# Branch and output projections of a hybrid layer as three float32r passes, with their splits between the merges

## The chip, the cores and the metric

The kernel runs on one core of a Trainium2 chip. The metric is the device time of one execution in microseconds; before the change the median of three runs is 1143.91 us (1143.75 to 1143.92).

## The reference

One layer over 256 tokens of width 1024, all in float32. One input projection gives queries, keys, values and a forget gate for an attention of eight heads, the channels of a pooling branch and of a state-space branch, and three gates per channel. The part that is changed joins the branches:

```
gates  = sigmoid(g)                                   # (256, 3, 1024)
merged = (gates[0] * (y_a @ w_branch_a)               # 512 -> 1024
        + gates[1] * (y_b @ w_branch_b)               # 256 -> 1024
        + gates[2] * (y_c @ w_branch_c))              # 256 -> 1024
mix = merged @ w_out                                  # 1024 -> 1024
x = layer_norm(alpha * x + mix)
x = layer_norm(alpha * x + moe(x))                    # top 4 of 32 experts
```

The mixture of experts reads all weights of all 32 experts, 384 chunks of 1 MiB. They are nearly all of the 438 MB that the kernel loads.

## The kernel before

**The ring.** SBUF holds 24 slots of 128x2048 float32, 1 MiB each. Weights come as chunks, one to a slot, in the order in which they are used: the input projection, then the eight chunks of the branch weights (`CH_BR`) and the output weights (`CH_WO`) in turn, then the experts. A slot that is released (`release`, `done`, `drop`) is at once given to the next chunk by `load_more` (L109), which puts one load into the queue of SyncE. That queue works in order, so a load waits for those ahead of it, and for the last reader of its slot. A buffer that isn't a chunk (the branch inputs, three tiles of gates, x itself) takes a slot with `keep` and gives it back with `drop`. Twelve slots are working space of the trunk at first; three of them (`f_spl`) hold the parts of split weights.

**Splits.** For the value, pooling and gate projections (the list `SPLIT`) a weight half of 128x1024 is split in two: ScalarE copies it as float32r (L235), VectorE subtracts that from the original (L236), and `mm3` (L250 to L252) multiplies in three float32r matmuls: high by high, high by low, low by high. Every projection of a half calls `split_next` behind its matmuls, which writes the parts three halves ahead, into the buffer that was just read.

**Stages.** Up to 156 us the trunk projects; attention, pooling and the state-space scan run on the other engines between. Then comes the part around the change. `branch(d)`, for d from 0 to 7, makes 128 of the 1024 merged channels: eight float32 products with the branch inputs `yv(k)` (L770) in PSUM tiles `pab` and `pcc`, and on VectorE the merge with the gates (L779, L780, L784, L785) into a tile `m`. `mixk` multiplies one `m` with its rows of the output weights, in four float32 products of 512 columns (L791) that add up in four PSUM tiles `mix` over d. The order in the code is branch 0, branch 1, mix 0, branch 2, mix 1, and so on, with the last two mixes at the end. In between stand the router's weights (GpSimd, L799), their sum over the rows (VectorE, L802), and the load of an activation table for Sqrt (ScalarE, L823). The layer norm and the routing follow, and from 224 us on the experts, two at a time, in 16 rounds of 24 chunks.

Of the kernel before, what the change touches and what calls it, by code (L numbers as in the profile page):

```python
# [17 lines left out]
S = 256  # L18
# [36 lines left out]
CH_V = [6, 7]  # L55
CH_UP = 8
CH_G = list(range(9, 21))
CH_BR = [21, 23, 25, 27]
CH_WO = [22, 24, 26, 28]
N_TRUNK = 29  # L60


@with_exitstack
def hybrid_layer(ctx: ExitStack, tc: tile.TileContext, wt, wm, pa, pb, pc, xin, bu, lnp, b_down, out):
    nc = tc.nc
    pe, act, dve, pool, sp = nc.tensor, nc.scalar, nc.vector, nc.gpsimd, nc.sync
    TT, TS, STT = dve.tensor_tensor, dve.tensor_scalar, dve.scalar_tensor_tensor
# [51 lines left out]
    def chunk(i):  # L119
        return chunks[i][0]  # L120

    def done(i):
        f = chunks.pop(i)[1]
        release(f)
# [4 lines left out]
    def a_(n):  # L129
        return pa_sb[:, PA[n][0]:PA[n][1]]  # L130
# [12 lines left out]
    epst = con.tile([128, 2], F32)  # L143
# [3 lines left out]
    junk = scr[:, 0:1]  # L147
# [47 lines left out]
    big = {}  # L195
# [10 lines left out]
    def drop(name):  # L206
        release(big.pop(name)[1])
# [2 lines left out]
    def gate_tile(i, n=1):  # L210
        return big[f"gates{i // 8}"][0].rearrange("p (u t) -> p u t", u=8)[:, i % 8:i % 8 + n]

    def yv(k, n=1):
        return big["y"][0].rearrange("p (k t) -> p k t", k=8)[:, k:k + n]

    def work(f):
        return place(f).rearrange("p (i q t) -> p i q t", i=4, q=2)

    SPLIT = CH_V + [CH_UP] + CH_G
    jobs = [(c, h) for c in SPLIT for h in range(2)]
    js = {"emitted": 0, "used": 0}
    parts = {}

    def split_next():
        j = js["emitted"]
        if j >= len(jobs):
            return
        js["emitted"] += 1  # L230
        ci, h = jobs[j]
        src = chunk(ci)[:, h * 1024:(h + 1) * 1024]
        t = place(f_spl[j % 3], F32R)
        hi, lo = t[:, 0:1024], t[:, 1024:2048]
        act.activation(out=hi, in_=src, func=ACTF.Copy)  # L235
        TT(lo, src, hi.bitcast(F32), op=ALU.subtract)  # L236
        parts[j] = (hi, lo)
        if h:
            done(ci)

    def split(ci, h):
        j = js["used"]
        js["used"] += 1
        assert jobs[j] == (ci, h)
        while js["emitted"] <= j:
            split_next()
        return parts.pop(j)

    def mm3(out, whi, wlo, ahi, alo, first, last):
        pe.matmul(out, whi, ahi, start=first, stop=False)  # L250
        pe.matmul(out, whi, alo, start=False, stop=False)  # L251
        pe.matmul(out, wlo, ahi, start=False, stop=last)  # L252
# [146 lines left out]


    def proj(ci, half, dst):
        if ci in SPLIT:
            hi, lo = split(ci, half)
            for k in range(8):
                mm3(dst, hi[:, k * 128:(k + 1) * 128], lo[:, k * 128:(k + 1) * 128], xhi[:, k], xlo[:, k], k == 0, k == 7)
            split_next()
        else:
            w = chunk(ci)[:, half * 1024:half * 1024 + 1024]
            for k in range(8):
                pe.matmul(dst, w[:, k * 128:(k + 1) * 128], xt3[:, k], start=(k == 0), stop=(k == 7))  # L410
            if half:
                done(ci)

    def pair_tile():
        return pm.tile([128, 2, S], F32, tag="m", name="pm")
# [90 lines left out]
    def s5_sigmoid():  # L506
        y, t, g, sg = s5st["post"]
        hb = sm("hb", 2)
        TS(hb, a_("b_glu"), 0.5, None, op0=ALU.mult)
        for m in range(2):  # L510
            act.activation(out=sg[:, m], in_=s5st["glu"][:, m], func=ACTF.Tanh, scale=0.25, bias=hb[:, m:m + 1])
        STT(t, sg, 1.0, g, op0=ALU.add, op1=ALU.mult)
        TS(yv(6, 2), t, 0.25, None, op0=ALU.mult)
        release(f_s0)


# [21 lines left out]
    def pool_out():  # L538
        mx = s5st["mx"]
        pp = pst.tile([128, 2, S], F32, tag="t", name="pp")  # L540
        wp = b_("w_pool").rearrange("p (j d) -> p j d", j=2)
        for j in range(2):
            pe.matmul(pp[:, j, :], wp[:, j, :], mx[:, j, :], start=True, stop=True)
        for j in range(2):
            TS(yv(4 + j)[:, 0], pp[:, j], a_("p_scale")[:, j:j + 1], None, op0=ALU.mult)
        release(f_s1)


# [43 lines left out]
    def att_pv(i):  # L592
        po = pst.tile([128, S], F32, tag="t", name="po")
        for part in range(2):
            for q in range(2):
                h = 2 * i + q
                PT = ast["T", h]
                o = po[64 * q:64 * q + 64]
                v = vsb[:, part, h * 64:(h + 1) * 64]
                if part == 0:  # L600
                    pe.matmul(o, v, PT[:, 0:256], start=True, stop=False)
                else:
                    pe.matmul(o[:, 128:256], v, PT[:, 256:384], start=False, stop=True)
        act.activation(out=yv(i)[:, 0], in_=po, func=ACTF.Copy)


    pus = pair_tile()
# [40 lines left out]
    def at(n, f, *a):  # L648
        side.setdefault(n, []).append((f, a))
# [46 lines left out]
    at(21, s5_out, 2)  # L696
    at(25, s5_out, 3)
    steps(s5_fwd, 0, 7, 7, 8, 8, 9, 9, 10, 10)
    at(6, keep, "y")
    at(9, keep, "gates0")  # L700
    steps(s5_fwd, 1, 11, 11, 12, 12, 13, 13, 14, 14)
    steps(s5_fwd, 2, 15, 15, 16, 16, 17, 17, 18, 18)
# [16 lines left out]
    for i in range(4):  # L719
        p = pair_tile()  # L720
# [14 lines left out]
    for g in range(12):  # L735
        if g in (3, 7):
            keep(f"gates{g // 4 + 1}")
        p = pair_tile()
# [4 lines left out]
    ph1.close()  # L743
    release(f_xhi)
    release(f_xlo)
    for f in f_spl:
        release(f)


    late = ctx.enter_context(tc.tile_pool(name="late", bufs=1, reuse_waits="tile"))  # L750
# [1 line left out]
    rbias = late.tile([128, 2, NE], F32)  # L752
    wrp = ExitStack()
    wr2 = wrp.enter_context(tc.tile_pool(name="wrp", bufs=1, side="right", reuse_waits="tile")).tile([128, 2, 8, NE], F32, name="wr2")
# [3 lines left out]
    pbr = ps2.enter_context(tc.tile_pool(name="pbr", bufs=2, space=PSUM, reuse_waits="tile"))  # L758
    pmx = ps2.enter_context(tc.tile_pool(name="pmx", bufs=1, space=PSUM, reuse_waits="tile"))
    wk2 = ps2.enter_context(tc.tile_pool(name="wk2", bufs=2, reuse_waits="tile"))  # L760
    mix = [[pmx.tile([128, 512], F32, name=f"mix{t}{n}") for n in range(2)] for t in range(2)]
    mst = {}

    def branch(d):
        w = chunk(CH_BR[d // 2])[:, d % 2 * 1024:d % 2 * 1024 + 1024]
        pab = pbr.tile([128, 2, S], F32, tag="ab", name="pab")
        pcc = pbr.tile([128, S], F32, tag="c", name="pcc")
        for dst, k0, k1 in ((pab[:, 0], 0, 4), (pab[:, 1], 4, 6), (pcc, 6, 8)):
            for k in range(k0, k1):
                pe.matmul(dst, w[:, k * 128:(k + 1) * 128], yv(k)[:, 0], start=(k == k0), stop=(k == k1 - 1))  # L770
        if d % 2:
            done(CH_BR[d // 2])

        t = wk2.tile([128, 3, S], F32, tag="mg", name="mg")
        if d == 5:
            STT(t[:, 0:1], gate_tile(15), 1.0, pab[:, 0:1], op0=ALU.add, op1=ALU.mult)
            STT(t[:, 1:2], gate_tile(16), 1.0, pab[:, 1:2], op0=ALU.add, op1=ALU.mult)
        else:
            STT(t[:, 0:2], gate_tile(3 * d, 2), 1.0, pab, op0=ALU.add, op1=ALU.mult)  # L779
        STT(t[:, 2:3], gate_tile(3 * d + 2), 1.0, pcc[:, None], op0=ALU.add, op1=ALU.mult)  # L780
        if d in (2, 5, 7):
            drop(f"gates{(d - 1) // 3 if d > 2 else 0}")
        m = wk2.tile([128, S], F32, tag="m", name="m", bufs=3)
        TT(t[:, 0], t[:, 0], t[:, 1], op=ALU.add)  # L784
        TT(m, t[:, 0], t[:, 2], op=ALU.add)  # L785
        mst[d] = m

    def mixk(*parts):
        for k, t, n in parts:
            w = chunk(CH_WO[k // 2])[:, k % 2 * 1024 + n * 512:k % 2 * 1024 + n * 512 + 512]  # L790
            pe.matmul(mix[t][n], mst[k][:, t * 128:(t + 1) * 128], w, start=(k == 0), stop=(k == 7))  # L791
            if (k % 2, t, n) == (1, 1, 1):
                done(CH_WO[k // 2])


    def router_weights():
# [2 lines left out]
            pool.tensor_tensor(wr2[:, i], wr2[:, 1], l1[:, 8 * i:8 * i + 8, None].to_broadcast([128, 8, NE]), op=ALU.mult)  # L799

    def router_reduce():
        dve.tensor_reduce(rbias, wr2.rearrange("p a k e -> p a e k"), axis=AX.X, op=ALU.add)  # L802

    def router_sums():
        pr = pbr.tile([128, S], F32, tag="c", name="prb")
# [6 lines left out]
    for k in range(7):  # L812
        if k == 1:
            keep("z")
        branch(k + 1)
        if k == 1:
            z = big["z"][0].rearrange("p (t d) -> p t d", t=2)
            sp.dma_start(out=z, in_=xin)
            router_weights()
        if k == 3:  # L820
            router_reduce()
        if k == 4:
            act.activation(out=junk, in_=epst[:, 0:1], func=ACTF.Sqrt)  # L823
            router_sums()
        if k == 6:
            drop("y")
        if k < 6:
            mixk(*[(k, t, n) for t in range(2) for n in range(2)])
    mixk((6, 0, 0), (6, 0, 1), (6, 1, 0), (7, 0, 0), (7, 0, 1), (6, 1, 1), (7, 1, 0), (7, 1, 1))


    ps3 = ExitStack()
# [513 lines left out]
```

## Time and profile before

| | |
|---|---|
| median of three runs | 1143.91 us |
| the profiled execution | 1143.99 us, its span 1142.0 us |
| PE busy | 1122.2 us (98%) |
| VectorE busy | 300.7 us (26%) |
| ScalarE busy | 184.8 us (16%) |
| GpSimd busy | 10.8 us (1%) |
| loaded | 438.04 MB, mean 384 GB/s |

Busy shares are means over the whole span. The stages differ: the trunk up to about 222 us, and the experts, which are four fifths of the time. A wait that matters must be looked for in its own stage.

### The profile page before, as it was taken

The numbers are of one execution on the slowest core, as the hardware profiler recorded it, in microseconds if no ns is written. First come the engines' busy times: TensorE is split into PE (matmuls) and PEld (weight loads), VectorE is DVE, ScalarE is ACT, GpSimd is POOL, SyncE is SP. The second block draws the span as 40 slices with busy tenths as digits, with TensorE's granted clock in tenths as the row PEclk, the third lists the DMA queues.
The fourth block names the chain that finished last, engine by engine and source line by source line (L and its number), as shares of the span: only waits on it lengthen the run. The fifth ranks groups of instructions, "written<-read, shape, count | busy, mean of one in ns | idle before, by whom it ended". The sixth has DMA issues, their size and how long they took to land. (4 is left out here: it accounts for less than half of the span.)

```text
span 1142.0 us, 13355 instructions
## 1 busy us (share of the span) xinstructions
PE 1122.2 (98%) x5535; PEld 518.0 (45%) x5535; DVE 300.7 (26%) x710; ACT 184.8 (16%) x389; POOL 10.8 (1%) x14
## 2 busy tenths in 40 slices
PE   9999999999999999999999999999999999999997
PEld 6888986633434343434343434343434343434332
DVE  4798633420302020212111111111111111111132
ACT  4555410301111010101010101010101010101002
POOL 0000000000000000000000000000000000000101
PEclk9999999999999999999999999999999999999999
DMA  9923596599999999999999999999999999999992
GB/s 370 388 96 133 236 360 250 221 415 427 427 427 426 426 426 426 426 427 427 427 427 426 427 426 426 421 427 426 427 427 426 428 426 427 426 426 426 412 425 97
DMA packets 63048, 438.04 MB, mean 384 GB/s; under 512 B 7012, under 2 KB 7524, under 8 KB 10632
## 3 DMA queue, kind: packets, MB, share of 16 engines
q1 hardware_dynamic: 62064, 435.46, 91.5%
q10 hardware_dynamic: 920, 1.69, 0.4%
q8 instruction: 45, 0.74, 0.2%
q14 instruction: 19, 0.16, 0.0%
HBM read 436.07 MB, written 1.05 MB: 383 GB/s over the span
## 5 line engine op out<-in xcount | busy, mean ns | idle before, releaser
L1030 PE MATMUL hu<-w,xg 128*64 128x512 f32 x2048 | 471.6, 596 | 6.4 <-DMA w<-in_wm_dram 6.3
L1030 PEld LDWEIGHTS hu<-w,xg 128*64 128x64 f32 x2048 | 155.7, 137 | 309.6 <-issue 278.7
L1030 PE MATMUL py<-w,at 128*64 128x512 f32 x1024 | 231.3, 597 | 0.0
L1002 DVE TENSOR_SCALAR s<-hu 128x256 f32<-128x256 f32 x64 | 27.0, 423 | 567.9 <-PE hu L1030 567.9
L1030 PEld LDWEIGHTS py<-w,at 128*64 128x64 f32 x1024 | 70.1, 136 | 136.3 <-issue 130.6
L1013 ACT ACTIVATE at<-pta 128x256 f32<-128x256 f32 x64 | 24.6, 384 | 408.3 <-PE pta L1012 408.3
L1039 PE MATMUL hu<-bup,pc_sb 128*64 128x512 f32 x256 | 67.5, 605 | 0.0
L1019 PE MATMUL acc<-y,gT 128*128 128x512 f32 x128 | 63.5, 618 | 1.5 <-ACT y L1047 1.5
L250 PE MATMUL pm<-w,w 128*128 128x256 f32 x208 | 60.6, 292 | 0.8 <-ACT vsb L643 0.8
L967 PE MATMUL pg<-oh,x 128*128 128x128 f32 x512 | 59.9, 275 | 0.0
L251 PE MATMUL pm<-w,w 128*128 128x256 f32 x208 | 58.8, 283 | 0.0
L252 PE MATMUL pm<-w,w 128*128 128x256 f32 x208 | 58.8, 283 | 0.0
L967 PEld LDWEIGHTS pg<-oh,x 128*128 128x128 f32 x512 | 58.4, 192 | 0.1
L1003 ACT ACTIVATE hu<-s 128x256 f32<-128x256 f32 x64 | 24.6, 385 | 166.0 <-DVE s L1002 166.0
L1047 ACT ACTIVATE y<-py 128x512 f32<-128x512 f32 x32 | 19.1, 597 | 190.8 <-PE py L1030 190.8
L236 DVE TENSOR_TENSOR w<-w,w 128x1024 fp32r<-128x1024 f32 x30 | 36.5, 1220 | 19.3 <-ACT w L235 19.2
L250 PEld LDWEIGHTS pm<-w,w 128*128 128x128 f32 x208 | 39.8, 191 | 3.8 <-issue 1.7
L1019 PEld LDWEIGHTS acc<-y,gT 128*128 128x128 f32 x128 | 21.7, 189 | 42.9 <-issue 39.7
L251 PEld LDWEIGHTS pm<-w,w 128*128 128x128 f32 x208 | 39.8, 192 | 0.1
L252 PEld LDWEIGHTS pm<-w,w 128*128 128x128 f32 x208 | 39.8, 191 | 0.0
L235 ACT ACTIVATE w<-w 128x1024 fp32r<-128x1024 f32 x30 | 31.6, 1058 | 35.4 <-PE pm L252 25.2
L971 ACT ACTIVATE xg<-pg,pc_sb 128x128 f32<-128x128 f32 x64 | 29.3, 458 | 48.1 <-DVE xg L973 48.1
(318 smaller groups left out, 687.1 us busy)
## 6 DMA issues: line engine op xcount, KB each, us to landing
w<-in_wm_dram SPq DMA_DIRECT2D x382, 1024.0 KB, 19.6
w<-in_wt_dram SPq DMA_DIRECT2D x26, 1024.0 KB, 10.3
w<-in_wm_dram SPq DMA_DIRECT2D x8, 256.0 KB, 13.3
w<-in_wt_dram SPq DMA_DIRECT2D x4, 256.0 KB, 6.4
w<-in_wt_dram ACTq DMA_DIRECT2D x4, 256.0 KB, 6.3
w<-in_wt_dram SPq DMA_DIRECT2D x2, 512.0 KB
w<-in_xin_dram SPq DMA_DIRECT2D x1, 1024.0 KB, 7.8
w<-in_pb_dram SPq DMA_DIRECT2D x1, 896.0 KB, 8.7
```

Source lines behind the costliest of these rows:

```text
L235: act.activation(out=hi, in_=src, func=ACTF.Copy)
L236: TT(lo, src, hi.bitcast(F32), op=ALU.subtract)
L250: pe.matmul(out, whi, ahi, start=first, stop=False)
L251: pe.matmul(out, whi, alo, start=False, stop=False)
L252: pe.matmul(out, wlo, ahi, start=False, stop=last)
L967: pe.matmul(pg[:, b], x1[:, t, k * 128:(k + 1) * 128], oh[:, t], start=(t == 0), stop=(t == 1))
L971: act.activation(out=xg[:, k], in_=pg[:, b], func=ACTF.Identity, scale=l1[:, k:k + 1], bias=l1[:, 8 + k:9 + k])
L1002: TS(xg, hu[:, 0:256], 7.0, None, op0=ALU.min)
L1003: act.activation(out=th, in_=xg, func=ACTF.Tanh, scale=0.851)
L1019: pe.matmul(accs[t][n], gT[:, t * 128:(t + 1) * 128], y, start=first, stop=True, skip_group_check=True)
L1030: pe.matmul(dst[64 * e:64 * e + 64], lhs[:, k, 64 * e:64 * e + 64], w[:, k % 4], start=first and k == 0, stop=(k == 7))
L1039: pe.matmul(hu[64 * e:64 * e + 64], ident[:, i:i + 1].to_broadcast([128, 64]), bup, start=True, stop=False)
```

## The change

The branch and the output projections now also go through `mm3` or its like: three float32r passes over high and low parts in place of one float32 product. The branch inputs are kept as two tiles, `yhi` and `ylo`, the merged channels as `mh` and `ml`, and the sixteen halves of the branch and output chunks join the list of splits, in the order branch 0, branch 1, output 0, branch 2, output 1 and on. A chunk is released when both its halves are split, the three split buffers at the end of the mixes. The sum of the router weights moves from VectorE to GpSimd, and the table load for Sqrt from the middle of the stage to its last merge.

```diff
+    for d in range(8 + LAG):                          # LAG = 1
+        if d in (0, 1, 2, 3, 4, 5, 6, 7):
+            jobs.append((CH_BR[d // 2], d % 2))
+        if d - LAG in (0, 1, 2, 3, 4, 5, 6, 7):
+            jobs.append((CH_WO[(d - LAG) // 2], (d - LAG) % 2))
...
+    def split_hi():
...
+            act.activation(out=parts[j][0], in_=chunk(ci)[:, h * 1024:(h + 1) * 1024], func=ACTF.Copy)
+            return j
+
+    def split_lo(j):
...
+            TT(lo, chunk(ci)[:, h * 1024:(h + 1) * 1024], hi.bitcast(F32), op=ALU.subtract)
+            half_done(ci)
...
-        act.activation(out=yv(i)[:, 0], in_=po, func=ACTF.Copy)
+        act.activation(out=yh(i)[:, 0], in_=po, func=ACTF.Copy)
+        TT(yl(i)[:, 0], po, yh(i)[:, 0].bitcast(F32), op=ALU.subtract)
...
-    at(6, keep, "y")
+    at(6, keep, "yhi", F32R)
+    at(7, keep, "ylo", F32R)
...
-    for f in f_spl:
-        release(f)
...
-                pe.matmul(dst, w[:, k * 128:(k + 1) * 128], yv(k)[:, 0], start=(k == k0), stop=(k == k1 - 1))
+                    mm3(dst, hi[:, ks], lo[:, ks], yh(k)[:, 0], yl(k)[:, 0], k == k0, k == k1 - 1)
...
+            ahead = split_hi()
...
+            TT(t[:, 0], t[:, 0], t[:, 2], op=ALU.add)
+            act.activation(out=mh, in_=t[:, 0], func=ACTF.Copy)
+            split_lo(ahead)
+            TT(ml, t[:, 0], mh.bitcast(F32), op=ALU.subtract)
...
+                pe.matmul(mix[t][n], m[:, ts], hi[:, ns], start=(k == 0), stop=False)
+                pe.matmul(mix[t][n], m[:, ts], lo[:, ns], start=False, stop=False)
+                pe.matmul(mix[t][n], ml[:, ts], hi[:, ns], start=False, stop=(k == 7))
+                if (t, n) == (1, 1):
+                    split_next()
...
-        dve.tensor_reduce(rbias, wr2.rearrange("p a k e -> p a e k"), axis=AX.X, op=ALU.add)
+        pool.tensor_tensor(half, wr2[:, :, 0:4], wr2[:, :, 4:8], op=ALU.add)
+        pool.tensor_tensor(half[:, :, 0:2], half[:, :, 0:2], half[:, :, 2:4], op=ALU.add)
+        pool.tensor_tensor(rbias, half[:, :, 0], half[:, :, 1], op=ALU.add)
...
+    for j in (3, 2, 1):
+        release(f_spl[(len(jobs) - j) % 3])
```

On VectorE the merges of branches 1 and 2 stood one behind the other before; `pab` and `pcc` are the products, `w` slots of the ring (here the gates), `mg` the merge's work tile:

```order
L779 SCALAR_TENSOR_TENSOR mg<-w_537,pab 128x512
L780 SCALAR_TENSOR_TENSOR mg<-w_537,pcc 128x256
L784 TENSOR_TENSOR mg<-mg 128x256
L785 TENSOR_TENSOR m<-mg 128x256
L779 SCALAR_TENSOR_TENSOR mg<-w_537,pab 128x512
L780 SCALAR_TENSOR_TENSOR mg<-w_1006,pcc 128x256
L784 TENSOR_TENSOR mg<-mg 128x256
L785 TENSOR_TENSOR m<-mg 128x256
```

The same place on VectorE in the changed kernel, where L256 is the subtraction that makes the low part of a weight half of 128x1024:

```order
L815 SCALAR_TENSOR_TENSOR mg<-w_536,pab 128x512
L816 SCALAR_TENSOR_TENSOR mg<-w_536,pcc 128x256
L819 TENSOR_TENSOR mg<-mg 128x256
L823 TENSOR_TENSOR mg<-mg 128x256
L256 TENSOR_TENSOR w_1741<-w_1082,w_1741 128x1024
L826 TENSOR_TENSOR ml<-mg,mh 128x256
L256 TENSOR_TENSOR w_1767<-w_1154,w_1767 128x1024
L815 SCALAR_TENSOR_TENSOR mg<-w_536,pab 128x512
L816 SCALAR_TENSOR_TENSOR mg<-w_1007,pcc 128x256
L819 TENSOR_TENSOR mg<-mg 128x256
L823 TENSOR_TENSOR mg<-mg 128x256
L256 TENSOR_TENSOR w_1798<-w_1156,w_1798 128x1024
```

Two subtractions of weights now stand with each merge, one between its sums and its low part, one ahead of the next merge.

In the queue of SyncE, the loads around the router weights (`in_pc`) and x (`in_xin`) before; `w23` is slot 23, and slots 14, 13 and 12 are the three split buffers:

```order
L109 DMA w23_1632<-in_wm_dram 128x2048
L109 DMA w22_1634<-in_wm_dram 128x2048
L109 DMA w14_1636<-in_wm_dram 128x2048
L109 DMA w13_1638<-in_wm_dram 128x2048
L109 DMA w12_1640<-in_wm_dram 128x2048
L756 DMA wr2_1650<-in_pc_dram 128x256
L109 DMA w11_1691<-in_wm_dram 128x2048
L818 DMA w8_1716<-in_xin_dram 128x2048
L109 DMA w1_1727<-in_wm_dram 128x2048
```

The same queue in the changed kernel, from the load into slot 22 to the one behind x, and the last ones ahead of the experts' own slots:

```order
L111 DMA w22_1651<-in_wm_dram 128x2048
L779 DMA wr2_1661<-in_pc_dram 128x256
L111 DMA w3_1752<-in_wm_dram 128x2048
L111 DMA w21_1770<-in_wm_dram 128x2048
L881 DMA w8_1803<-in_xin_dram 128x2048
L111 DMA w20_1866<-in_wm_dram 128x2048
...
L111 DMA w0_2101<-in_wm_dram 128x2048
L111 DMA w13_2127<-in_wm_dram 128x2048
L111 DMA w12_2129<-in_wm_dram 128x2048
L111 DMA w14_2131<-in_wm_dram 128x2048
L111 DMA w8_2267<-in_wm_dram 128x2048
```

The three split buffers have moved from ahead of the router weights to the end of the stage, next to x's own slot. Counted over the queue, the expert loads ahead of the router weights, between these and x, and from x to the load into x's slot were 12, 1 and 10, and are 9, 2 and 12.

## Rows read from the trace of the kernel before

**Rows 1.** The page: busy time of PE, and the span in 40 slices.
```profile
PE 1122.2 (98%) x5535; PEld 518.0 (45%) x5535; DVE 300.7 (26%) x710; ACT 184.8 (16%) x389; POOL 10.8 (1%) x14
...
PEclk9999999999999999999999999999999999999999
DMA  9923596599999999999999999999999999999992
GB/s 370 388 96 133 236 360 250 221 415 427 427 427 426 426 426 426 426 427 427 427 427 426 427 426 426 421 427 426 427 427 426 428 426 427 426 426 426 412 425 97
```

**Rows 2.** Waits of PE: us in total, times, longest.
```profile
PE hu L1030 <- DMA w<-in_wm_dram: 6.3, 15, 1.2
PE pz L1188 <- PEq L1098: 2.7, 1, 2.7
```

**Rows 3.** Busy time by engine in four stretches, with clock and DMA.
```profile
core 0: us, PE busy (x) PEld busy (x) DVE busy (x) ACT busy (x) POOL busy (x), PEclk, DMA share, GB/s
60.00:156.00 96.00, 95.52 (x786) 87.89 (x786) 70.84 (x116) 44.95 (x86) 0.00 (x0) 1.00 0.50 187
156.10:211.60 55.50, 55.50 (x198) 36.83 (x198) 18.50 (x43) 3.56 (x6) 1.23 (x2) 1.00 0.75 288
...
222.20:227.50 5.30, 5.30 (x30) 2.31 (x31) 2.22 (x9) 1.40 (x4) 0.00 (x0) 1.00 0.00 0
227.50:240.00 12.50, 12.50 (x62) 4.11 (x58) 2.36 (x6) 1.05 (x3) 0.00 (x0) 1.00 0.90 370
240.00:1115.00 875.00, 867.11 (x3986) 326.32 (x3984) 152.31 (x364) 90.47 (x216) 4.94 (x4) 1.00 1.01 426
```

**Rows 4.** Waits of SyncE's queue, 155 to 235 us.
```profile
SPq L109 <- PE hu L1030: 12.7, 2, 10.1
```

**Rows 5.** SyncE's queue in order of time, 216.5 to 228.5 us: start, us.
```profile
217.07 11.27 SPq L109 DMA_DIRECT2D w<-in_wm_dram  x3
```

**Rows 6.** PE in order of time where the experts begin.
```profile
223.00 1.08 PE L1039 MATMUL hu<-bup,pc_sb 128*64 128x512 f32 x4
223.91 7.04 PE L1030 MATMUL hu<-w,xg 128*64 128x512 f32 x32
```

**Rows 7.** PE in order of time: one branch, one mix, the next branch.
```profile
159.62 2.75 PE L770 MATMUL pab<-w,w 128*128 128x256 f32 x12
162.22 1.03 PE L770 MATMUL pcc<-w,w 128*128 128x256 f32 x4
163.08 3.60 PE L791 MATMUL mix<-w,m 128*128 128x512 f32 x8
166.51 2.75 PE L770 MATMUL pab<-w,w 128*128 128x256 f32 x12
```

**Rows 8.** PE in order of time: gate projections in float32r, 51 matmuls.
```profile
150.05 0.28 PE L250 MATMUL pm<-w,w 128*128 128x256 f32 x1
...
156.05 0.28 PE L252 MATMUL pm<-w,w 128*128 128x256 f32 x1
```

**Rows 9.** PE in order of time: value projection in float32r, 20 matmuls.
```profile
53.10 0.39 PE L637 MATMUL pv<-w,w 128*128 128x512 f32 x1
...
57.41 0.39 PE L638 MATMUL pv<-w,w 128*128 128x512 f32 x1
```

**Rows 10.** Groups by line, 60 to 156 us: busy, mean ns | idle before.
```profile
L236 DVE TENSOR_TENSOR w<-w,w 128x1024 fp32r<-128x1024 f32 x24 | 29.3, 1220 | 17.8 <-ACT w L235 17.7
L235 ACT ACTIVATE w<-w 128x1024 fp32r<-128x1024 f32 x23 | 24.3, 1058 | 32.0 <-PE pm L252 25.2 <-issue 6.2 <-ACT P L573 0.7
```

**Rows 11.** Waits of VectorE, 56 to 156 us.
```profile
DVE w L236 <- ACT w L235: 17.8, 12, 2.8
```

**Rows 12.** Groups by line: a merge, and a copy of 128x256 from PSUM.
```profile
L779 DVE SCALAR_TENSOR_TENSOR mg<-w,pab 128x512 f32<-128x512 f32 x7 | 4.8, 688 | 34.3 <-PE pab L770 34.3
L785 DVE TENSOR_TENSOR m<-mg 128x256 f32<-128x256 f32 x8 | 3.4, 426 | 0.3
L780 DVE SCALAR_TENSOR_TENSOR mg<-w,pcc 128x256 f32<-128x256 f32 x8 | 3.4, 422 | 1.3 <-PE pcc L770 1.1
L784 DVE TENSOR_TENSOR mg<-mg 128x256 f32<-128x256 f32 x8 | 3.4, 420 | 0.0
L604 ACT ACTIVATE w<-po 128x256 f32<-128x256 f32 x4 | 1.4, 362 | 0.0
```

**Rows 13.** Groups by line: the table load, the router weights and their sum.
```profile
L823 ACT ACT_TABLE_LOAD x1 | 1.3, 1283 | 0.0
L799 POOL TENSOR_TENSOR wr<-wr,pc_sb 128x256 f32<-128x256 f32 x2 | 1.2, 617 | 172.4 <-DMA wr<-in_pc_dram 172.3
L802 DVE TENSOR_REDUCE rbias<-wr 128x64 f32<-128x512 f32 x1 | 1.0, 1046 | 0.0
```

More of the change, by code (lines that the diff above doesn't have):

```diff
@@ L60 @@
 N_TRUNK = 29
+LAG = 1
 @with_exitstack
@@ L211, in gate_tile, with yh, yl, half_done @@
         return big[f"gates{i // 8}"][0].rearrange("p (u t) -> p u t", u=8)[:, i % 8:i % 8 + n]
-    def yv(k, n=1):
-        return big["y"][0].rearrange("p (k t) -> p k t", k=8)[:, k:k + n]
+    def yh(k, n=1):
+        return big["yhi"][0].rearrange("p (k t) -> p k t", k=8)[:, k:k + n]
+    def yl(k, n=1):
+        return big["ylo"][0].rearrange("p (k t) -> p k t", k=8)[:, k:k + n]
     def work(f):
         return place(f).rearrange("p (i q t) -> p i q t", i=4, q=2)
-    SPLIT = CH_V + [CH_UP] + CH_G
-    jobs = [(c, h) for c in SPLIT for h in range(2)]
+    jobs = [(c, h) for c in CH_V + [CH_UP] + CH_G for h in range(2)]
+    for d in range(8 + LAG):
[3 more added lines that the diff above has]
+            jobs.append((CH_WO[(d - LAG) // 2], (d - LAG) % 2))
     js = {"emitted": 0, "used": 0}
     parts = {}
-    def split_next():
[L227 to L239, printed above, removed]
+    halves = {}
+    def half_done(ci):
+        halves[ci] = halves.get(ci, 0) + 1
+        if halves[ci] == 2:
+            done(ci)
+    def split_hi():
+        j = js["emitted"]
+        if j < len(jobs):
+            js["emitted"] += 1
+            ci, h = jobs[j]
+            t = place(f_spl[j % 3], F32R)
+            parts[j] = t[:, 0:1024], t[:, 1024:2048]
+            act.activation(out=parts[j][0], in_=chunk(ci)[:, h * 1024:(h + 1) * 1024], func=ACTF.Copy)
+            return j
+    def split_lo(j):
+        if j is not None:
+            ci, h = jobs[j]
+            hi, lo = parts[j]
+            TT(lo, chunk(ci)[:, h * 1024:(h + 1) * 1024], hi.bitcast(F32), op=ALU.subtract)
+            half_done(ci)
+    def split_next():
+        split_lo(split_hi())
     def split(ci, h):
@@ L401, in proj @@
     def proj(ci, half, dst):
-        if ci in SPLIT:
+        if (ci, half) in jobs:
             hi, lo = split(ci, half)
@@ L410, in proj @@
                 pe.matmul(dst, w[:, k * 128:(k + 1) * 128], xt3[:, k], start=(k == 0), stop=(k == 7))
-            if half:
-                done(ci)
+            half_done(ci)
     def pair_tile():
@@ L512, in s5_sigmoid @@
         STT(t, sg, 1.0, g, op0=ALU.add, op1=ALU.mult)
-        TS(yv(6, 2), t, 0.25, None, op0=ALU.mult)
+        act.activation(out=yh(6, 2), in_=t, func=ACTF.Copy, scale=0.25)
+        STT(yl(6, 2), t, 0.25, yh(6, 2).bitcast(F32), op0=ALU.mult, op1=ALU.subtract)
         release(f_s0)
@@ L544, in pool_out @@
         for j in range(2):
-            TS(yv(4 + j)[:, 0], pp[:, j], a_("p_scale")[:, j:j + 1], None, op0=ALU.mult)
+            ps = a_("p_scale")[:, j:j + 1]
+            act.activation(out=yh(4 + j)[:, 0], in_=pp[:, j], func=ACTF.Copy, scale=ps)
+            STT(yl(4 + j)[:, 0], pp[:, j], ps, yh(4 + j)[:, 0].bitcast(F32), op0=ALU.mult, op1=ALU.subtract)
         release(f_s1)
@@ L760, in hybrid_layer @@
     wk2 = ps2.enter_context(tc.tile_pool(name="wk2", bufs=2, reuse_waits="tile"))
+    rsum = wk2.tile([128, 256], F32, name="rsum", bufs=1)
     mix = [[pmx.tile([128, 512], F32, name=f"mix{t}{n}") for n in range(2)] for t in range(2)]
@@ L764, in branch @@
     def branch(d):
-        w = chunk(CH_BR[d // 2])[:, d % 2 * 1024:d % 2 * 1024 + 1024]
+        ci, h = CH_BR[d // 2], d % 2
+        exact = (ci, h) in jobs
+        if exact:
+            hi, lo = split(ci, h)
+        else:
+            w = chunk(ci)[:, h * 1024:h * 1024 + 1024]
         pab = pbr.tile([128, 2, S], F32, tag="ab", name="pab")
@@ L769, in branch @@
             for k in range(k0, k1):
-                pe.matmul(dst, w[:, k * 128:(k + 1) * 128], yv(k)[:, 0], start=(k == k0), stop=(k == k1 - 1))
-        if d % 2:
-            done(CH_BR[d // 2])
+                ks = slice(k * 128, (k + 1) * 128)
+                if exact:
+                    mm3(dst, hi[:, ks], lo[:, ks], yh(k)[:, 0], yl(k)[:, 0], k == k0, k == k1 - 1)
+                else:
+                    raise NotImplementedError
+        if exact:
+            ahead = split_hi()
+        else:
+            ahead = None
+            half_done(ci)
         t = wk2.tile([128, 3, S], F32, tag="mg", name="mg")
@@ L782, in branch @@
             drop(f"gates{(d - 1) // 3 if d > 2 else 0}")
-        m = wk2.tile([128, S], F32, tag="m", name="m", bufs=3)
         TT(t[:, 0], t[:, 0], t[:, 1], op=ALU.add)
-        TT(m, t[:, 0], t[:, 2], op=ALU.add)
-        mst[d] = m
+        if (CH_WO[d // 2], d % 2) in jobs:
+            mh = wk2.tile([128, S], F32R, tag="mh", name="mh", bufs=3)
+            ml = wk2.tile([128, S], F32R, tag="ml", name="ml", bufs=3)
+            TT(t[:, 0], t[:, 0], t[:, 2], op=ALU.add)
+            act.activation(out=mh, in_=t[:, 0], func=ACTF.Copy)
+            split_lo(ahead)
+            TT(ml, t[:, 0], mh.bitcast(F32), op=ALU.subtract)
+            mst[d] = mh, ml
+        else:
+            m = wk2.tile([128, S], F32, tag="m", name="m", bufs=3)
+            TT(m, t[:, 0], t[:, 2], op=ALU.add)
+            mst[d] = m, None
+    ws = {}
     def mixk(*parts):
         for k, t, n in parts:
[L790 to L793, printed above, removed]
+            ci, h = CH_WO[k // 2], k % 2
+            ts, ns = slice(t * 128, (t + 1) * 128), slice(n * 512, (n + 1) * 512)
+            m, ml = mst[k]
+            if ml is None:
+                w = chunk(ci)[:, h * 1024:h * 1024 + 1024]
+                pe.matmul(mix[t][n], m[:, ts], w[:, ns], start=(k == 0), stop=(k == 7))
+                if (t, n) == (1, 1):
+                    half_done(ci)
+            else:
+                if k not in ws:
+                    ws[k] = split(ci, h)
+                hi, lo = ws[k]
+                pe.matmul(mix[t][n], m[:, ts], hi[:, ns], start=(k == 0), stop=False)
+                pe.matmul(mix[t][n], m[:, ts], lo[:, ns], start=False, stop=False)
+                pe.matmul(mix[t][n], ml[:, ts], hi[:, ns], start=False, stop=(k == 7))
+                if (t, n) == (1, 1):
+                    split_next()
     def router_weights():
@@ L801, in router_reduce @@
     def router_reduce():
-        dve.tensor_reduce(rbias, wr2.rearrange("p a k e -> p a e k"), axis=AX.X, op=ALU.add)
+        half = rsum.rearrange("p (a k e) -> p a k e", a=2, k=4)
+        pool.tensor_tensor(half, wr2[:, :, 0:4], wr2[:, :, 4:8], op=ALU.add)
+        pool.tensor_tensor(half[:, :, 0:2], half[:, :, 0:2], half[:, :, 2:4], op=ALU.add)
+        pool.tensor_tensor(rbias, half[:, :, 0], half[:, :, 1], op=ALU.add)
     def router_sums():
@@ L822, in hybrid_layer @@
         if k == 4:
-            act.activation(out=junk, in_=epst[:, 0:1], func=ACTF.Sqrt)
             router_sums()
         if k == 6:
-            drop("y")
+            act.activation(out=junk, in_=epst[:, 0:1], func=ACTF.Sqrt)
+            drop("yhi")
+            drop("ylo")
         if k < 6:
```

## The prediction

> **What bounds the kernel now.** I read the page first. PE is busy for 1122.2 of 1142.0 us, its clock digit is 9 in all 40 slices, and the DMA digits are 9 from slice 9 on, at 425 to 428 GB/s [rows 1]. Two resources are thus near their limit at once, and the question is which of them sets the end. The list of PE's waits answers a part: it waits 6.3 us in all for expert weights, in 15 short waits, and the next largest wait is 2.7 us, once [rows 2]. Then the windows: in the stage that is changed, 156.1 to 211.6 us, PE is busy for 55.50 of 55.50 us, DVE for 18.50, ACT for 3.56, and the DMA engines move 288 GB/s of some 426. From 222.2 to 227.5 the DMA engines move nothing, and from 240 to 1115 they never pause [rows 3]. The queue of SyncE says why: it issues three loads from 217.07 to 228.34, and waits up to 10.1 us for PE to be done with an expert chunk [rows 4, 5]. The ring is full when the expert stage begins (PE's first expert products are at 223.91 [rows 6]), and the first free slot comes with the end of the pause, at about 227.5.
>
> So the end is set by this: the first expert slot becomes free, the DMA engines start at full rate, and 360 more loads of 1 MiB, at 426 GB/s 2.46 us each, follow. An earlier trunk on PE moves that start, and with it everything behind, by its own amount, on one condition: the ring must again be full, or nearly, by then.
>
> **The matmuls.** A branch step of eight float32 products (128x256) goes from 159.62 to 163.08, 3.46 us, and a mix step of four (128x512) from 163.08 to 166.51, 3.43 us [rows 7]. The step pair takes 6.89 us, and there are eight pairs. In their place come 24 float32r matmuls of 256 columns and 12 of 512. Both shapes stand in the trace before: fifty steps of the gate projections take 156.05 - 150.05 = 6.00 us, 0.120 us each [rows 8], and nineteen of the value projection 57.41 - 53.10 = 4.31 us, 0.227 us each, with the same pattern of two operands and the same 128x128 weights [rows 9]. New pair: 24 x 0.120 = 2.88 plus 12 x 0.227 = 2.72, 5.60 us. Saved: 1.29 us a pair, 10.3 us for eight.
>
> The Trainium skill (FP8 and Floating Point Precision, section TensorE Precision Notes) says that true FP32 takes four passes through the array. By that rule three passes would leave three quarters of 55.1 us and save 13.8; the trace does not agree with so much, since a float32r pass takes 0.120 and not a quarter of 3.46 / 8 (0.108). I take the rows.
>
> **The parts of the weights.** Sixteen halves are split, each with an ACT copy (1.058 us) and a DVE subtraction (1.220 us) [rows 10]. In a pair that is 2.12 us of ACT and 2.44 of DVE. A merge is 0.69 + 0.42 + 0.42 + 0.43 = 1.96 us of DVE [rows 12], and the new low part of its result one more of 128x256, some 0.43; the high part is an ACT copy of some 0.36, as L604 [rows 12]. DVE then has 2.44 + 1.96 + 0.43 = 4.83 us of work in a pair of 5.60, ACT 2.48. Both fit, though DVE has only 0.8 us left, so the order matters. I follow it in the order rows on DVE: the subtraction for a buffer that branch d has freed stands behind the two sums of merge d and ahead of its low part; the one for the buffer that a mix has freed stands ahead of the next merge. Take the end of mix 0 as zero. ACT copies 0.1 to 1.2, DVE subtracts to 2.4; the two-branch sums of branch 2 are ready at 18 x 0.120 = 2.16, so that merge begins 0.3 late; its third product is ready at 2.9, merged by 4.3; the second subtraction ends at 5.5 and the low part at 5.9. PE wants that low part in mix 2, after branch 2, mix 1 and branch 3, 2.88 + 2.72 + 2.88 = 8.5. Slack 2.5 us. Each part has three buffers' distance and is written some 3 us before PE comes to it. Only the first mix is tight: just branch 1 stands between merge 0 and mix 0, the low part is due 2.88 + 2 x 0.227 = 3.3 us after branch 0 and is ready after about 2.9. Term: 0, bounds 0 and, if DVE's few tenths of delay in a pair all reached PE, 8 x 0.3 = 2.4 us.
>
> **The three first splits** (both halves of the first branch chunk, one of the first output chunk) fall into the last gate projections. DVE and ACT are busy there and before for 70.84 and 44.95 of 96 us, and DVE waits 17.8 us for ACT's copies, which wait 25.2 for PE to free a buffer [rows 3, 10]: both run as far ahead as three buffers let them. That hides the low parts of the branch inputs too (four PSUM subtractions of some 0.43, and one or two longer forms in place of a scaling each, under 3 us in all). Without that cover they would cost 3 us at most; I take 0.
>
> **GpSimd and the table.** The reduction of the router weights (1.046 us of DVE) becomes three GpSimd sums of 256, 128 and 64 elements; two products of 256 elements took 0.617 each there, so I estimate under 1.9 us in all, some 8 us ahead of the matmul that reads it [rows 13]. It relieves DVE by 1.05 us once: 0, as DVE isn't the bound. The Sqrt table load (1.283 us [rows 13]) now stands behind the last merge's copy, some 5 us ahead of the first square: 0; uncovered it would cost 1.3.
>
> **The ring.** Here the change takes something away. The low parts of the branch inputs hold one more slot from the projections to the last branch, and the three split buffers, given back at 157 before, are given back after the last mix. The order rows on SyncE show it: ahead of the router weights 9 expert loads stand instead of 12, between these and the load of x 2 instead of 1, and behind x, up to the one that takes x's own slot, 12 instead of 10. On the other side branch and output chunks are freed at their split. I date the last loads by the new steps: branch 7 ends at 156.1 + 8 x 2.88 + 6 x 2.72 = 195.5, the mixes at 201, and the slot of z (217.07 before [rows 5]) at 206.8. Eight loads are asked for from about 195 on; eight times 2.46 is 19.7, and I estimate 2 us to start, from the 370 GB/s of the first 12.5 us after the pause (1.6 us lost) [rows 3]. They are in at about 217. The first expert slot is free at 227.5 - 10.3 = 217.2. So the ring is full just in time: the idle 5.3 us of before are used up, and nothing is lost. Term: 0; bounds: the start without a pause gains up to 1.6 us, and if loads were so late that the DMA engines ran 5 us behind, 5 of the 10.3 would be gone.
>
> **Sum.** From the profiled 1143.99 us (1142.0 of span and 2.0 around it, 0.1 above the median of the runs): 1143.99 - 10.3 + 0 = 1133.7 us. The bounds of the hidden terms: 1133.7 - 1.6 = 1132.1, and with 2.4 of DVE and some of the ring 1137 to 1138.
>
> **Rivals.** *The expert loads keep the end.* DMA at its limit for 875 us speaks for it. Against it: the start of that stretch is released by PE, as the pause shows. If the 12 loads behind x came 5 us too late, the gain would be 5: 1139. From 10.3 us too late on there is no gain.
>
> *The parts pace PE in a part of the pairs.* DVE at 4.83 of 5.60 speaks for it; the slack of 2.5 us against it. With half the gain lost, 1139.
>
> *Slower.* DVE works in order, and the merge stands behind a subtraction that waits for ACT, which waits for PE to give up the buffer. DVE's longest such wait before was 2.8 us, with three buffers as now [rows 11]. If PE in turn waits for that merge, each pair loses 2.8 and saves 1.29: 8 x 1.5 = 12 us slower, 1156. It decides from a wait of 1.29 us a pair. Against it: mix k reads merge k with a whole branch, and from k = 1 also a mix, between them, and in the projections, where VectorE works in the same way, PE lost 0.48 us in 96 [rows 3].
>
> *Three of four passes.* If a float32r pass took a quarter of a float32 product, in both shapes: 1143.99 - 13.8 = 1130.2. Against it stand both spacings [rows 8, 9]. It is the rule of the Trainium skill that is named above.
>
> **Chances.** The forecast 0.76, late loads 0.06, parts that pace PE 0.08, three of four passes 0.03, slower 0.07. About 0.2% (2.3 us) is what can be told from no change. All but the slower case and a small share of the two partial ones lie beyond it: faster 0.91, same 0.02, slower 0.07. The range takes the bounds of the hidden terms and three passes: 1130 to 1138.
>
> **What would show it.** Right: float32r rows at spacings of 0.12 and 0.227 us in a stage of 45 us instead of 55.5; PE without a wait there; x1's transposes near 201; first expert products near 213.6; DMA without a pause between 195 and the end. Wrong: PE waits for DVE or ACT at the first product of a branch or the third of a mix (the parts pace it); a stage of 45 us but an end that came less than 10 us earlier, with more PE waits for expert weights than 6.3 us (the ring); a stage of 55 us or more (slower).

## The result, and the profile after

The changed kernel takes 1134.86 us (median of 19 runs, 1134.45 to 1135.61 and one at 1144.66) against 1143.92 us (19 runs). The ratio is 0.9925, with a 95% interval from 0.9918 to 0.9932: 9.1 us faster. The forecast was 10.3 us, 1133.7. The profiled execution has a span of 1132.7 us where it was 1142.0.

The page of the changed kernel, the same lines as [rows 1]:

```profile
PE 1109.9 (98%) x5631; PEld 520.3 (46%) x5631; DVE 322.8 (28%) x737; ACT 206.1 (18%) x416; POOL 13.3 (1%) x17
...
PEclk9999999999999999999999999999999999999999
DMA  9823686999999999999999999999999999999992
GB/s 362 366 83 129 238 347 258 389 426 426 428 426 426 428 426 426 427 426 427 427 426 426 426 427 426 422 427 426 426 427 427 426 426 428 426 426 427 413 425 95
```

PE has more matmuls to run and is busy for 12 us less. The clock digit is 9 throughout, as before. In the row of GB/s the slice in which the DMA engines reach their full rate has moved up: the eighth slice is now at 389 and the ninth at 426, where they were at 221 and 415.

The stretches that answer to [rows 3], cut at the new stage's own ends (PE's first branch matmul and its first transpose behind the mixes):

```profile
156.40:202.00 45.60, 45.60 (x293) 41.18 (x292) 36.42 (x63) 21.13 (x26) 3.75 (x5) 1.00 0.79 298
202.00:207.00 5.00, 4.24 (x65) 3.48 (x64) 4.63 (x19) 3.84 (x9) 1.53 (x2) 1.00 1.01 424
207.00:217.00 10.00, 10.00 (x107) 7.76 (x105) 5.07 (x23) 4.63 (x10) 0.00 (x0) 1.00 1.00 419
217.00:220.00 3.00, 3.00 (x18) 1.01 (x14) 0.00 (x0) 0.00 (x0) 0.00 (x0) 1.00 0.44 126
```

The stage is 45.60 us long and PE is busy in all of it, although VectorE is now busy for 36.42 of it and ScalarE for 21.13 (18.50 and 3.56 of 55.5 before). From 202 to 217 the DMA engines are full. Ahead of the first expert slot they lose some 1.7 us (0.44 of 3 us busy), where before they moved nothing for the 5.3 us of [rows 3].

PE in order of time in the changed kernel, one branch and one mix, with the first matmul of what follows; the columns are start and duration:

```profile
159.28 0.28 PE L271 MATMUL pab<-w,w 128*128 128x256 f32 x1
...
162.16 0.39 PE L849 MATMUL mix<-w,mh 128*128 128x512 f32 x1
...
164.96 0.28 PE L271 MATMUL pab<-w,w 128*128 128x256 f32 x1
...
167.82 0.39 PE L849 MATMUL mix<-w,mh 128*128 128x512 f32 x1
```

A branch takes 162.16 - 159.28 = 2.88 us, as forecast (3.46 before [rows 7]). A mix takes 164.96 - 162.16 = 2.80 us, where 2.72 were forecast: 0.233 us for each of its twelve matmuls, and not the 0.227 of the value projection [rows 9].

The experts begin with PE's bias matmuls; the first products with expert weights, in the second row, were dated at 213.6:

```profile
213.79 1.08 PE L1105 MATMUL hu<-bup,pc_sb 128*64 128x512 f32 x4
214.70 7.04 PE L1096 MATMUL hu<-w,xg 128*64 128x512 f32 x32
```

PE's waits in the changed kernel from 156 to 214 us, which is the whole list for the stage and for the routing behind it:

```profile
PE pl L956 <- DVE lq L936: 0.8, 1, 0.8
```

No wait stands in the stage. This one, in the routing, was 0.3 us before:

```profile
PE pl L890 <- DVE lq L870: 0.3, 1, 0.3
```

VectorE and GpSimd, in order of time, at that place in the changed kernel:

```profile
204.55 0.15 DVE L941 RECIPROCAL rs<-rs 128x1 f32<-128x1 f32 x1
204.73 0.16 DVE L942 TENSOR_TENSOR mv<-mv,rs 128x1 f32<-128x1 f32 x1
204.93 0.68 DVE L943 SCALAR_TENSOR_TENSOR lb<-rbias,mv 128x32 f32<-128x32 f32 x1
205.54 0.47 DVE L936 COPY lq<-pq 128x128 f32<-128x128 f32 x2
...
204.81 1.53 POOL L970 TENSOR_SCALAR x<-w,mv,rs 128x512 f32<-128x512 f32 x2 [33.20 <-DVE rs L941]
```

GpSimd's normalization of x (L970) starts 0.12 us ahead of VectorE's small operation on `rbias`, which then takes 0.68 us. Behind that stand the copies `lq` for which PE waits. In the kernel before, GpSimd was released one VectorE instruction later (by L876, and not by the reciprocal ahead of it), and the same operation took 0.25 us:

```profile
214.38 1.54 POOL L904 TENSOR_SCALAR x<-w,mv,rs 128x512 f32<-128x512 f32 x2 [40.29 <-DVE mv L876]
...
214.43 0.25 DVE L877 SCALAR_TENSOR_TENSOR lb<-rbias,mv 128x32 f32<-128x32 f32 x1
```

The same shows in the stage itself. VectorE and GpSimd in the changed kernel, from 168 to 172 us:

```profile
168.38 0.76 DVE L819 TENSOR_TENSOR mg<-mg 128x256 f32<-128x256 f32 x1
169.18 0.84 DVE L823 TENSOR_TENSOR mg<-mg 128x256 f32<-128x256 f32 x1
169.95 1.48 DVE L256 TENSOR_TENSOR w<-w,w 128x1024 fp32r<-128x1024 f32 x1
...
168.94 0.80 POOL L863 TENSOR_TENSOR rsum<-wr 128x256 f32<-128x256 f32 x1
169.82 0.53 POOL L864 TENSOR_TENSOR rsum<-rsum 128x128 f32<-128x128 f32 x1
170.42 1.19 POOL L865 TENSOR_TENSOR rbias<-rsum 128x64 f32<-128x64 f32 x1
```

The two sums of this merge take 0.76 and 0.84 us, where 0.42 is usual [rows 12], and the subtraction 1.48 and not 1.22. VectorE loses 0.34 + 0.42 + 0.26 = 1.0 us there, about as much as the reduction that was taken from it (1.046 [rows 13]). How much of it is due to the sums on GpSimd is told by the run with the sum on VectorE again, below. The Trainium skill (SBUF — State Buffer, section Who interferes with whom) says that a VectorE instruction with two SBUF inputs contends with a GpSimd instruction that reads SBUF, and that the order of issue decides which of them is blocked. These rows agree that the two contend. They don't settle the order: in the kernel before, too, GpSimd's normalization starts ahead of VectorE's operation (by 0.05 us), and that takes 0.25 us.

### The profile page after: what moved, and what is told of

Same layout as the page of the kernel before. It is cut to its first block, busy times and chain, and to the rows that moved or that the text cites. A ratio compares the mean times of both kernels' runs of the same rounds, so it can differ in the third digit from the quotient of the medians.

```text
span 1132.7 us, 13619 instructions
## 1 busy us (share of the span) xinstructions
PE 1109.9 (98%) x5631; PEld 520.3 (46%) x5631; DVE 322.8 (28%) x737; ACT 206.1 (18%) x416; POOL 13.3 (1%) x17
## 3 DMA queue, kind: packets, MB, share of 16 engines
HBM read 436.07 MB, written 1.05 MB: 386 GB/s over the span
## 5 line engine op out<-in xcount | busy, mean ns | idle before, releaser
L256 DVE TENSOR_TENSOR w<-w,w 128x1024 fp32r<-128x1024 f32 x46 | 56.3, 1225 | 27.5 <-ACT w L249 27.3
L249 ACT ACTIVATE w<-w 128x1024 fp32r<-128x1024 f32 x46 | 48.6, 1059 | 54.0 <-PE pm L273 25.1
```

The costliest lines, as they stand in the source:

```text
L249: act.activation(out=parts[j][0], in_=chunk(ci)[:, h * 1024:(h + 1) * 1024], func=ACTF.Copy)
L256: TT(lo, chunk(ci)[:, h * 1024:(h + 1) * 1024], hi.bitcast(F32), op=ALU.subtract)
```

## The experiments

Times are medians. The kernel before, run beside these kernels, is at 1143.88 to 1143.99 (at 1144.17 beside the last one). A stage is counted in each trace from PE's first branch matmul to its first transpose.

**Only the branches, and only the output projection.** One half of the change each.

```diff
# only the branches
-        if d - LAG in (0, 1, 2, 3, 4, 5, 6, 7):
+        if d - LAG in ():
...
+            split_lo(ahead)
# only the output projection
-        if d in (0, 1, 2, 3, 4, 5, 6, 7):
+        if d in ():
...
+                    pe.matmul(dst, w[:, ks], yh(k)[:, 0], start=(k == k0), stop=(k == k1 - 1))
```

In the second kernel the branch inputs stay one float32 tile, without `ylo`.

> Only the branch projections go in three float32r passes; the output projection stays one float32 product of the merged channels. Theory A (spacings alone, the end moves with the trunk one to one): 8 x (3.46 - 2.88) = 4.6 us faster than the kernel before, about 1139.3. Theory B (A, but each change between float32 and float32r on PE costs about 0.1 us, as 0.22 instead of 0.12 at the first float32r matmul behind a float32 one shows in the projections): two changes a pair, 1.5 us less gain, about 1140.8. Rival (the splits on ScalarE and VectorE are what costs the missing microsecond): with half the splits the stage would come out shorter than its matmul spacings say only if PE waits vanished; there are none to vanish, so no difference from A.

> Only the output projection goes in three float32r passes; the branch projections stay float32 products of unsplit inputs, and one slot of the ring less is held. Theory A (spacings alone): 8 x (3.43 - 12 x 0.234) = 5.0 us faster than before, about 1138.9. Theory B (a change of type costs about 0.1 us): 3.5 us faster, about 1140.4. If A holds for both this run and the run with only the branches, their gains add up to the whole gain of 9.1 to 9.4; under B they add up to about 6.5.

Measured: 1140.30 us (ratio 0.9961, 0.9944 to 0.9977) and 1140.65 us (0.9966, 0.9949 to 0.9983). PE's rows at the two ends of the stage, of the kernel with only the branches:

```profile
155.94 0.28 PE L271 MATMUL pab<-w,w 128*128 128x256 f32 x1
...
206.63 1.58 PE L920 MATMUL tpx<-pc_sb,w 128*128 128x128 f32 x13
```

And of the kernel with only the output projection:

```profile
156.20 0.38 PE L796 MATMUL pab<-w,w 128*128 128x256 f32 x1
...
206.49 1.69 PE L909 MATMUL tpx<-pc_sb,w 128*128 128x128 f32 x14
```

The stages are 50.69 and 50.29 us long, the one of before 211.49 - 156.17 = 55.32. They gain 4.63 and 5.03 us, and together 9.66, as both do in one kernel (55.32 - 45.60 = 9.72). So the traces bear out A for the stage: the halves add up, and no price of a change of type on PE shows in them. The times gained, 3.6 and 3.3 us, add up to 6.9 and not to 9.1, and look more like B; but their intervals reach from 2.6 to 6.4 and from 1.9 to 5.8 us and hold both. The profile of the first kernel is of its fastest run (1138.92, where the twelve reach up to 1140.62), so it can't tell what its other runs lose. In the one profile of the second kernel the experts take 0.8 us longer, from PE's first expert matmul to the end, than in that of the kernel before. Nearly all of that lies behind the start of the last round of experts; here is PE's first gather of that round, in the second kernel and in the kernel before:

```profile
1040.05 3.74 PE L1023 MATMUL pg<-oh,x 128*128 128x128 f32 x32
```

```profile
1044.71 1.50 PE L967 MATMUL pg<-oh,x 128*128 128x128 f32 x12
```

From there to the end pass 1138.1 - 1040.05 = 98.05 us and 1142.0 - 1044.71 = 97.29. Over all traces of this case this last stretch takes 97.1 to 98.1 us, so single profiles differ by some tenths that no change explains. What makes the medians of the two halves together 2.2 us less than the whole is open.

**The subtraction ahead of the merge.** The order of the splits undone.

```diff
-            ahead = split_hi()
+            split_next()
+            ahead = None
```

> The whole change, but the subtraction that makes the low part of the next weights stands ahead of the merge on VectorE, not between its sums and its low part. Theory (slack of 2.5 us in all pairs but the first): only the first mix comes late, by about 1.7 us, since just one branch stands between it and its merge; 1136.5. Rival (the splits pace PE, their order is worth a stall in every pair): 8 x 1.7 = 13 us slower than the changed kernel, 1148, with PE waits for VectorE in each mix.

Measured: 1138.19 us (0.9944, 0.9927 to 0.9960), 3.3 us slower than the changed kernel. PE's waits in the stage:

```profile
PE mix L850 <- ACT mh L825: 3.0, 2, 1.7
```

There are two waits, and not eight. The first, 1.71 us, is the one expected, at the first mix. The second, 1.25 us, lies at branch 7's first mix, which I had left out: the code ends with two mixes without a branch between them, and there too the merge has little to stand behind. In between no wait stands: there the slack is real. The stage is 205.38 - 156.29 = 49.09 us long, 3.49 more than in the changed kernel, of which the two waits are 2.96. The order between the merges is worth 3.3 us, at the two ends of the stage.

**The sum on VectorE again.**

```diff
-        pool.tensor_tensor(half, wr2[:, :, 0:4], wr2[:, :, 4:8], op=ALU.add)
...
+        dve.tensor_reduce(rbias, wr2.rearrange("p a k e -> p a e k"), axis=AX.X, op=ALU.add)
```

> The whole change, but the sum of the router weights is one reduction on VectorE again. Theory (VectorE has slack there): the same time as the changed kernel within 0.3 us, 1134.9. VectorE's merge of branch 2, whose two sums took 0.76 and 0.84 us beside the GpSimd sums in the changed kernel, takes 0.42 and 0.42 again where GpSimd doesn't run. Rival (the move to GpSimd is part of the gain, because 1.05 us of VectorE stood before the merge): 1 us slower, 1135.9.

Measured: 1134.94 us (0.9912, 0.9880 to 0.9943, 6 runs), the same. The rows in the routing, VectorE and GpSimd:

```profile
204.77 0.26 DVE L939 SCALAR_TENSOR_TENSOR lb<-rbias,mv 128x32 f32<-128x32 f32 x1
...
204.73 1.54 POOL L966 TENSOR_SCALAR x<-w,mv,rs 128x512 f32<-128x512 f32 x2 [36.17 <-DVE mv L938]
```

GpSimd is released by the later instruction again, the operation takes 0.26 us, and PE comes from the mixes to the experts in 11.51 us, as before, and not in 11.79. In the stage, at the merge of branch 2:

```profile
168.23 0.60 DVE L818 TENSOR_TENSOR mg<-mg 128x256 f32<-128x256 f32 x1
168.87 0.42 DVE L822 TENSOR_TENSOR mg<-mg 128x256 f32<-128x256 f32 x1
169.21 1.22 DVE L256 TENSOR_TENSOR w<-w,w 128x1024 fp32r<-128x1024 f32 x1
...
167.23 1.32 POOL L858 TENSOR_TENSOR wr<-wr,pc_sb 128x256 f32<-128x256 f32 x2 [166.79 <-DMA wr<-in_pc_dram]
...
156.24:201.84 45.60, 45.60 (x293) 41.19 (x292) 36.49 (x64) 21.11 (x26) 1.24 (x2) 1.00 0.77 296
```

The second sum and the subtraction are back at 0.42 and 1.22 us, so GpSimd's sums were what made them longer. The first sum still takes 0.60: it stands beside GpSimd's products (L858), which both kernels have. VectorE is busy for 36.49 us of this stage with the reduction on it, and for 36.42 without. So the move to GpSimd takes 0.28 us in the routing, too little to show in the time, and gives none back in the stage.

**PE later by 5 us.**

```diff
-    stay_warm(46)
+    stay_warm(46 + 84)
```

> The changed kernel with 84 more of the small matmuls (0.059 us each) that PE runs while the routing is worked out: PE comes to the experts 5.0 us later, and nothing else changes. Theory (the end is the first expert slot's release plus a fixed time): 5.0 us slower than the changed kernel, 1139.9, with PE's waits for expert weights as before (about 7 us in all). Rival (the loads set the end by themselves, since the ring was filled only just in time): less than half of it shows, under 1137.4, and PE's waits shrink by what is missing.

Measured: 1139.59 us (0.9960, 0.9946 to 0.9973), 4.7 us slower than the changed kernel. The delay came out at 4.70 us (the 11.79 us from the mixes to the experts became 16.49), and PE's waits for expert weights are 6.9 us in all, as in the changed kernel. One to one: the loads didn't take up any of it.

**Two slots less.**

```diff
-    for j in (3, 2, 1):
+    for j in (3,):
         release(f_spl[(len(jobs) - j) % 3])
```

> The changed kernel, but two of the three split buffers are never given back to the ring: 22 slots for the experts. PE's own work is the same. Theory (DMA sets the end from the first free slot on): two loads fewer are in hand then, 2 x 2.46 = 4.9 us slower, 1139.8, and PE waits some 12 us for expert weights instead of 6.9. Rival (PE's work sets the end, the waits of 7 us are small and there is slack in the ring): under 1 us slower, 1135 to 1136.

Measured: 1139.60 us (0.9964, 0.9950 to 0.9977), 4.7 us slower: two loads at 2.46 us make 4.9. The list of PE's waits, though, rose from 6.9 us only to 7.6. Where the time went is seen in PE's gather at the start of a round of experts, each row the first of its round. In the changed kernel:

```profile
574.17 0.61 PE L1033 MATMUL pg<-oh,x 128*128 128x128 f32 x4
...
628.80 0.61 PE L1033 MATMUL pg<-oh,x 128*128 128x128 f32 x4
...
683.44 0.83 PE L1033 MATMUL pg<-oh,x 128*128 128x128 f32 x6
...
742.17 0.72 PE L1033 MATMUL pg<-oh,x 128*128 128x128 f32 x5
798.50 2.17 PE L1033 MATMUL pg<-oh,x 128*128 128x128 f32 x18
...
976.46 0.72 PE L1033 MATMUL pg<-oh,x 128*128 128x128 f32 x5
...
1035.40 0.83 PE L1033 MATMUL pg<-oh,x 128*128 128x128 f32 x6
```

And with two slots less, from the round that begins at 628.55 to the last one:

```profile
628.55 0.61 PE L1033 MATMUL pg<-oh,x 128*128 128x128 f32 x4
...
684.75 0.50 PE L1033 MATMUL pg<-oh,x 128*128 128x128 f32 x3
...
745.13 0.72 PE L1033 MATMUL pg<-oh,x 128*128 128x128 f32 x5
...
1039.89 3.29 PE L1033 MATMUL pg<-oh,x 128*128 128x128 f32 x28
```

A round takes 54.63 us while the loads are ahead. In the changed kernel the step comes after 683.44: the six rounds from there to 1035.40 take 58.66 us on average (58.73 and 56.33 for the first two), and 24 loads of 2.46 us are 59. With two slots less the round from 628.55 already takes 56.20, and the six behind it 59.19 on average. From there on PE goes at the pace of the DMA engines, in both.

**The first slots earlier.** The bias product of the first unit behind its weights' products, alone and with the sum on VectorE.

```diff
+        if early:                                  # round 0, unit 0
+            products(hu, N_TRUNK + 24 * p + 4 * n, xg, True, False)
         for e in range(2):
...
+        if not early:
             products(hu, N_TRUNK + 24 * p + 4 * n, xg, False)
```

> The changed kernel, but in the first unit of the first experts the bias product (0.91 us of PE) stands behind the weights' products instead of ahead of them: the first slots come free 0.9 us earlier, PE's work is the same. Theory: 0.9 us faster, 1134.0, PE's waits for expert weights down by as much. Rival (PE's work sets the end): no difference.

> The same, with the sum of the router weights on VectorE again, whose run showed the experts beginning 0.28 us sooner behind the mixes (x1's first half on GpSimd then no longer blocks VectorE's small operation there). Theory: 0.9 + 0.3 = 1.2 us faster than the changed kernel, 1133.7. Rival (only the one or the other counts): 1134.0 to 1134.6.

Measured: 1133.91 us (0.9910, 0.9895 to 0.9925, 4 runs) and 1134.57 us (0.9916, 0.9902 to 0.9929, 5 runs). The medians lie 0.95 and 0.3 us under the changed kernel, and the intervals overlap with its own. The spans of the two profiles, 1132.6 and 1132.5 us, stand beside 1132.7. In the first of them the last round of experts begins 0.58 us earlier (1034.82 and 1035.40), but the stretch behind it, 97.8 us, is 0.5 us longer, within what it varies by. This is not decided, and no version is shown to beat the changed kernel.

**The mixes pass by pass.**

```diff
+            for j, (l, r) in enumerate(((m, hi), (m, lo), (ml, hi))):
+                for _, t, n in parts:
+                    pe.matmul(mix[t][n], l[:, t * 128:(t + 1) * 128], r[:, n * 512:(n + 1) * 512], ...)
```

> The changed kernel, but the first six mixes go pass by pass over the four PSUM tiles (high by high for all four, then high by low, then low by high) in place of three passes for one tile after the other. In the changed kernel a 512-column float32r matmul follows the last one after 0.234 us, where the prediction took 0.227 from the value projection. Theory A (three matmuls in a row into one PSUM tile cost it): the spacing falls to 0.227, 12 x 0.007 x 6 = 0.5 us in all. Theory B (it doesn't hang on the order of the passes): 0.234 stays, and the stage of 45.6 us with it.

In one run, 1135.51 us, beside 1144.17 for the kernel before. The spacing within a mix stays at 0.234 us and the stage at 45.59 (45.60). B holds: the order over the PSUM tiles is not the cause. What makes a 512-column matmul follow after 0.234 us here and after 0.227 in the later part of the value projection is open.

## Why the prediction was right, point by point

*What sets the end.* Right, and now shown from two sides: PE later by 4.70 us makes the kernel slower by 4.7, two loads fewer by 4.7. From PE's first expert matmul to the end the profile has 1142.0 - 223.0 = 919.0 us before and 1132.7 - 213.8 = 918.9 after, so the gain of the trunk came through whole. What I read as the measure of how far the loads pace PE was too small: the 6.3 us of [rows 2] are only what PE's matmuls waited. PE's weight loads have a list of their own; their waits for expert weights, in the kernel before and in the changed one, in that order:

```profile
PEld hu L1030 <- DMA w<-in_wm_dram: 24.7, 33, 2.1
```

```profile
PEld hu L1096 <- DMA w<-in_wm_dram: 25.4, 33, 2.6
```

In the changed kernel this comes near to what the rounds lose, 6 x (58.66 - 54.63) = 24.2 us. But it isn't the measure either: with two slots less it stands at 25.2, though the rounds lose 28.9 us there (1.57 in the first and 6 x 4.56), 4.7 more, which is the whole of what that kernel is slower. Only the spacing of the rounds shows the loss.

*The matmuls.* The term of 10.3 us was mis-sized: the stage gained 9.72. The branch came out as forecast, the mix at 0.233 to 0.234 us a matmul where 0.227 was taken. 96 x 0.0065 = 0.6 us, all that is missing in the stage. The value projection's spacing was read from its later, faster part. Its first matmuls in the kernel before stand further apart:

```profile
45.19 0.40 PE L637 MATMUL pv<-w,w 128*128 128x512 f32 x1
...
47.50 0.39 PE L638 MATMUL pv<-w,w 128*128 128x512 f32 x1
```

That is ten steps in 2.31 us, 0.231 each. So the choice of rows explains a good half of the error at most, and the rest, from 0.231 to 0.2335, was in none of these rows.

*The parts of the weights.* Right: no wait of PE, with VectorE busy for 36.42 of 45.60 us. The first mix was named as the tight place; the last one is one too, and only the run with the other order showed it.

*GpSimd.* The term of 0 was wrong by a little: the move cost 0.28 us in the routing, by a way that was not in the list: the change of an early operation set another release for a later one, which then started further ahead of VectorE's. The three sums took 0.80 + 0.53 + 1.19 = 2.5 us, where under 1.9 were estimated, and no wait came of that. And VectorE was not relieved by 1.05 us but by 36.49 - 36.42 = 0.07.

*The ring.* Right in its result, a little off in time: the DMA engines were full from 202 to 217 us, and the last loads came in soon after 217. The pause was not quite used up, so the sign "DMA without a pause between 195 and the end" did not come true: the first free slot was dated too early. In the kernel before, SyncE's third load is issued at 228.34 [rows 5] and not at 227.5, and 9.2 us ahead of that is 219.1. No gain from a start without a pause showed.

*The sum.* In the profile 9.72 - 0.28 = 9.44 us. PE came to its first branch matmul 0.23 us later (156.40, 156.17), in which no effect of the change is shown: the other changed kernels begin that stage between 155.9 and 157.1. That leaves 9.2, at PE's first expert matmul 223.00 - 213.79 = 9.21. The median says 9.1. PE's first products with expert weights, dated at 213.6, came at 214.70, by the same three amounts (0.60 + 0.28 + 0.23 = 1.1).

*The rivals.* Late loads: no, the ring was full before the first slot came free, and the run with PE later says the same. Parts that pace PE: no, by the list of waits. Three of four passes: no, at spacings of 0.120 and 0.234 us. Slower: no; even the unfavourable order stalls PE twice and not eight times.

## What to carry to other kernels

Where two resources are near their limit, find the moment at which one begins to run without a pause, and ask what releases it: here PE's work ahead of that moment counted one to one, although the DMA engines paced the end. Take a duration for a new instruction from the whole of its nearest rows and not from their best part. To see how far loads pace an engine, take the spacing of the rounds that repeat, not a list of waits. Work that is moved to an idle engine can come back as a blocked instruction on the old one: check the durations beside it.

## What the runs showed of the hardware that was not expected

VectorE instructions with two SBUF inputs took 0.68 to 0.84 us instead of 0.25 to 0.42 beside GpSimd instructions that read SBUF, in the changed kernel. Whether VectorE was delayed hung on less than 0.1 us: GpSimd's normalization, started 0.05 us ahead of VectorE's operation in the kernel before, left it at 0.25 us, and started 0.12 us ahead it came with 0.68. GpSimd's own two operations took 1.54 and 1.53 us in these two cases. In the stage GpSimd was slow as well: its smallest sum, of 64 columns, took 1.19 us beside VectorE's subtraction, where the one of 128 columns ahead of it took 0.53.
